# A seven-product down projection: two sets of slots, weight parts parked in device memory, activations split per pair of k

## The chip, the cores and the metric

The kernel runs on one core of a Trainium2 chip, in one launch. The metric is the device time of that launch in microseconds; three runs of the kernel before are known. The core's engines are named as in the profile: PE (TensorE, with PEld for its weight loads), DVE (VectorE), ACT (ScalarE), POOL (GpSimd) and SP (SyncE), which here only issues DMAs.

## The reference

Two post-norm layers on a sequence of 256 positions with 2048 features, all in float32. Layer 0 mixes tokens with a gated spatial unit (gMLP), layer 1 with latent attention (MLA); a gated FFN with a causal convolution follows each.

```python
for i in range(DEPTH):                         # DEPTH = 2
    m = gmlp_mixer(x, ...) if i % 2 == 0 else mla_mixer(x, ...)
    x = layer_norm(ALPHA * x + m, ln_mix_g[i], ln_mix_b[i])
    f = conv_ffn(x, ffn_w_up[i], ffn_conv_w[i], ffn_conv_b[i], ffn_w_down[i])
    x = layer_norm(ALPHA * x + f, ln_ffn_g[i], ln_ffn_b[i])

def conv_ffn(x, w_up, conv_w, conv_b, w_down):  # w_up 2048 x 11008, w_down 5504 x 2048
    h = causal_depthwise_conv3(x @ w_up, conv_w) + conv_b
    a, g = jnp.split(h, 2, axis=-1)
    return (jax.nn.silu(g) * a) @ w_down
```

The gMLP's input projection is 2048 x 12288 (half of it u, half v), its output projection 6144 x 2048.

## The kernel before

**Products.** PE multiplies numbers of the type float32r. To keep float32's accuracy, every operand x is split into hi = x rounded to float32r (a copy on ACT) and lo = x - hi (a subtraction on DVE), and a product is three matmuls: hi by hi, lo by hi, hi by lo (prod_b, L284).

**Eight or seven products.** In the projections v, wo (the gMLP's output) and dn (an FFN's down projection), the weights come in chunks of one pair of k (two blocks of 128 rows) by 1024 columns, 1 MB. Both blocks of 128 positions use them, so a pair is a product of 2 x 2 blocks of activations by 2 x 2 blocks of weights (128 x 512). A "wide" pair does it in eight products (Banks.eight, L341), 24 matmuls. A "seven" pair does it in seven (Banks.seven, L348), 21 matmuls, with sums of weight blocks (ts, made on DVE at L122) and of activation blocks (combine, L209). Four banks (OWN) collect results that Banks.rest (L358) adds up after the last such pair of a half or group; the four others (DIRECT) take the rest.

**Order.** Feed (L69) owns the weights: a list of chunks in order of use. next() (L142) returns the split parts of one chunk, and before that issues loads up to four chunks ahead and splits up to two ahead. Loads go through SP's queue in that order. A wide chunk takes three slots (raw, wh, wl), a seven six (raw, ts, wh, wl, th, tl).

**Slots.** One set of 22 slots of 128 x 2048 words, "big", holds nearly everything: weights, the activations between the stages (pT and act, 8 k to a slot), their split parts, the split layer input (xhl, four slots), the residual (res, two slots), g and b of the norms. A slot is given back after its last use; who wants one waits. Smaller buffers are "t1" (8 of them) and "t2" (6).

**Stages.** v (6 groups of 8 chunks), u (12 groups of 4) with the gate, wo (2 halves of 24 pairs); a boundary: norm, transposes and the first group of the next product, while the last three or four chunks of the old one are still multiplied (boundary, L471); up (86 chunks in 22 groups), dn (2 halves of 22 units, the last of which is a single k), a boundary, MLA, a boundary, and up and dn of layer 1. BACK (L56) lists which pairs of wo and dn are sevens (7 and 6 a half) and the order of the second half. Sums (L370) makes the split activations, four k at a time (quad), and for a seven its four combinations (make), which serve both halves.

Of the kernel before, what the change touches and what calls it, by code (L numbers as in the profile page):

```python
# [8 lines left out]
F32 = mybir.dt.float32  # L9
# [6 lines left out]
P = 128  # L16
S = 256
# [42 lines left out]
def halves(n_k):  # L60

    one = [tuple(range(k, min(k + 2, n_k))) for k in range(0, n_k, 2)]
    two = []
    for q in BACK[n_k][1]:
        two += one[2 * q : 2 * q + 2][:: -1 if q in BACK[n_k][2] else 1]
    return [one, two]


class Feed:  # L69
# [3 lines left out]
    def __init__(self, nc, pool, chunks):  # L73
        self.nc, self.pool, self.chunks = nc, pool, chunks
# [19 lines left out]
    def _split(self):  # L94
        i = self.split
        cols, kind = self.chunks[i][1:]
# [5 lines left out]
        hi = self.pool.tile([P, 2048], F32R, tag="big", name=f"wh{i}")  # L102
        lo = self.pool.tile([P, 2048], F32R, tag="big", name=f"wl{i}")
# [14 lines left out]
    def _seven(self, i, raw):  # L118
# [4 lines left out]
        tile = lambda name, dt: self.pool.tile([P, 2048], dt, tag="big", name=f"{name}{i}")  # L123
# [8 lines left out]
        return wh, wl, th, tl  # L132

# [16 lines left out]
def trunk(ctx: ExitStack, tc: tile.TileContext, x, xT, gm_in, gm_wout, ffn_up, ffn_dn,  # L150
# [4 lines left out]
    big = ctx.enter_context(tc.tile_pool(name="big", bufs=22))  # L155
# [4 lines left out]
    def slot(shape, name, dt=F32):  # L160
        return big.tile(shape, dt, tag="big", name=name)
# [8 lines left out]
    chunks = []  # L170
# [6 lines left out]
    def back(w, n_k):  # L177

        for hf, units in enumerate(halves(n_k)):
            c = slice(hf * 1024, (hf + 1) * 1024)  # L180
            for u in units:
                if len(u) == 1:
                    chunks.append((w[u[0], :, c], 1024, "wide"))
                else:
                    chunks.append((w[u[0] : u[0] + 2, :, c].rearrange("k p c -> p k c"), 2048,
                                   "seven" if u[0] in BACK[n_k][0] else "wide"))

# [972 lines left out]
```

## Time and profile before

| | |
|---|---|
| median of 3 runs | 2493.01 us (2491.49 to 2493.38) |
| profiled execution | 2493.04 us, its span 2491.3 us |
| PE busy | 2475.7 us, 99% of the span |
| DVE busy | 1908.8 us, 77% |
| ACT busy | 1388.8 us, 56% |
| POOL busy | 2.9 us |
| DMA | 480 MB, 193 GB/s on average |
| granted TensorE clock | 0.999 |

Busy time is a share of the whole span, over stages with different limits; a row of windows gives it for one stage. A row of a group names the code line, the engine, the operation, what it writes from what it reads with the shape, how often it ran, its busy time and the mean of one in ns, and the time that the engine sat idle before it, with what ended that. Matmuls are pipelined, so their means overlap; the time of one is read from a run of them in the chain. A wait names who waited, for whom, and then the microseconds in total, the count and the longest.

### The profile page before, as it was taken

The page shows a single profiled execution, that of the slowest core. Times are in us where ns is not written, and L with a number is a line of the kernel's source. Part 1 is how long each engine was busy: PE and PEld are TensorE (multiplying, and loading weights), DVE is VectorE, ACT ScalarE, POOL GpSimd, SP SyncE. Part 2 cuts the span into 40 slices and gives each one's busy share as a digit, 9 for nine tenths or more (in the row PEclk, how much of TensorE's full clock was granted, in tenths as well). Part 3 has the DMA queues.
Part 4 walks back from the last instruction along what each step waited for, and adds up shares of the span by engine and source line. Part 5 has one row for each costly group of instructions (what it writes and reads, how often), then busy time and mean ns, then how long its engine had stood idle before and what let it go on. Part 6 is the DMA issues. An engine that isn't in the chain of part 4 may idle for free.

```text
span 2491.3 us, 32651 instructions
## 1 busy us (share of the span) xinstructions
PE 2475.7 (99%) x13028; PEld 2128.3 (85%) x13028; DVE 1908.8 (77%) x2553; ACT 1388.8 (56%) x1891; POOL 2.9 (0%) x17
## 2 busy tenths in 40 slices
PE   9999999999999999999999999999999999999998
PEld 7888888888888888888888888988888888888886
DVE  7999866678888777666778997866487676669897
ACT  6566544445565755554655566565565555546553
POOL 0000000000000000000000000000000000000000
PEclk9999999999999999999999999999999999999999
DMA  7555554555566655555546674444465455555554
GB/s 295 198 187 214 196 186 157 181 196 194 186 217 222 223 186 200 188 184 185 187 155 201 219 247 169 168 153 168 156 231 191 169 202 182 180 179 179 209 192 181
DMA packets 86456, 480.27 MB, mean 193 GB/s; under 512 B 7712, under 2 KB 8480, under 8 KB 46752
## 3 DMA queue, kind: packets, MB, share of 16 engines
q1 hardware_dynamic: 86304, 478.19, 54.4%
q8 instruction: 102, 1.67, 0.3%
q14 instruction: 50, 0.41, 0.1%
HBM read 476.07 MB, written 2.10 MB: 192 GB/s over the span
## 4 chain that ended last, share of the span: by engine, by line
PE 96%; DVE 2%; issue 1%; DMA 1%; ACT 0%; SPq 0%; DVEq 0%; ACTq 0%
PE up L167 37%; PE u L167 11%; PE dn_q L167 9%; PE dn_p L167 6%; PE wo_q L167 4%; PE v_q L167 4%; PE mo L167 4%; PE dn_e L167 3%; PE v_p L167 3%; PE wo_p L167 3%; PE upf L167 2%; PE wo_e L167 2%; PE v_e L167 1%; PE mkv L167 1%; PE kn L167 1%; PE mq L167 1%
## 5 line engine op out<-in xcount | busy, mean ns | idle before, releaser
L108 DVE TENSOR_TENSOR wl<-raw,wh 128x1024 fp32r<-128x1024 f32 (+3 forms) x651 | 899.8, 1407 | 158.6 <-ACT wh L107 115.5
L107 ACT CAST wh<-raw 128x1024 fp32r<-128x1024 f32 (+3 forms) x651 | 761.8, 1201 | 284.9 <-DVE wl L108 120.4
L167 PE MATMUL up<-xhl,wh 128*128 128x512 f32 x2624 | 611.0, 390 | 0.0
L167 PEld LDWEIGHTS up<-xhl,wh 128*128 128x128 f32 x2624 | 487.4, 188 | 97.8
L167 PEld LDWEIGHTS up<-xhl,wl 128*128 128x128 f32 x2624 | 325.8, 192 | 6.4
L167 PE MATMUL up<-xhl,wl 128*128 128x256 f32 x2624 | 328.1, 283 | 0.0
L115 ACT CAST th<-ts 128x1536 fp32r<-128x1536 f32 x116 | 121.1, 1051 | 118.6 <-DVE ts L122 103.9
L167 PE MATMUL u<-xhl,wh 128*128 128x512 f32 x768 | 183.8, 393 | 0.3 <-DVE h_u L313 0.2
L167 PEld LDWEIGHTS u<-xhl,wh 128*128 128x128 f32 x768 | 141.3, 188 | 30.8 <-PE s L167 2.1
L116 DVE TENSOR_TENSOR tl<-ts,th 128x1536 fp32r<-128x1536 f32 x116 | 138.6, 1219 | 5.3 <-ACT th L115 4.5
L115 ACT CAST wh<-raw 128x1536 fp32r<-128x1536 f32 x58 | 85.9, 1480 | 43.2 <-DMA raw<-in_ffn_dn_dram 15.2
L116 DVE TENSOR_TENSOR wl<-raw,wh 128x1536 fp32r<-128x1536 f32 x58 | 101.6, 1752 | 5.4 <-ACT wh L115 5.4
L167 PEld LDWEIGHTS u<-xhl,wl 128*128 128x128 f32 x768 | 95.6, 192 | 2.0
L167 PE MATMUL u<-xhl,wl 128*128 128x256 f32 x768 | 96.7, 283 | 0.0
L167 PE MATMUL mo<-wh,oT 128*128 128x512 f32 x256 | 82.9, 404 | 0.0
L122 DVE TENSOR_TENSOR ts<-ts,raw 128x512 f32<-128x512 f32 x116 | 79.8, 688 | 1.8
L167 PE MATMUL wo_q<-wh,woa 128*128 128x512 f32 x256 | 78.8, 389 | 0.0
L122 DVE TENSOR_TENSOR ts<-raw 128x1024 f32<-128x1024 f32 x58 | 70.8, 1220 | 4.6 <-PE u L167 1.6
L313 DVE TENSOR_TENSOR h_0a<-up,lo_0a 128x256 f32<-128x256 f32 x41 | 17.3, 421 | 72.7 <-ACT lo_0a L311 72.7
L313 DVE TENSOR_TENSOR h_1a<-up,lo_1a 128x256 f32<-128x256 f32 x41 | 17.3, 421 | 71.9 <-ACT lo_1a L311 71.9
L167 PE MATMUL dn_q<-wh,dn0a 128*128 128x512 f32 x232 | 71.7, 390 | 0.0
L167 PE MATMUL dn_q<-wh,dn1a 128*128 128x512 f32 x232 | 71.5, 389 | 0.0
(497 smaller groups left out, 3924.6 us busy)
## 6 DMA issues: line engine op xcount, KB each, us to landing
raw<-in_ffn_up_dram SPq DMA_DIRECT2D x172, 1024.0 KB, 4.7
raw<-in_gm_in_dram SPq DMA_DIRECT2D x93, 1024.0 KB, 4.7
raw<-in_ffn_dn_dram SPq DMA_DIRECT2D x84, 1024.0 KB, 5.1
raw<-in_gm_wout_dram SPq DMA_DIRECT2D x48, 1024.0 KB, 5.2
raw<-in_ml_out_dram SPq DMA_DIRECT2D x16, 1024.0 KB, 4.8
raw<-in_ml_b_dram SPq DMA_DIRECT2D x14, 1024.0 KB, 4.8
raw<-in_ml_kv_dram SPq DMA_DIRECT2D x5, 864.0 KB, 4.4
lng<-in_ln_rows_dram SPq DMA_DIRECT2D x4, 1024.0 KB, 5.0
```

The costliest lines, as they stand in the source:

```text
L107: self.nc.scalar.copy(hi[:, c], raw[:, c])
L108: self.nc.vector.tensor_tensor(lo[:, c], raw[:, c], hi[:, c].bitcast(F32), ALU.subtract)
L115: self.nc.scalar.copy(hi, raw)
L116: self.nc.vector.tensor_tensor(lo, raw, hi.bitcast(F32), ALU.subtract)
L122: add = lambda o, a, b: self.nc.vector.tensor_tensor(o, a, b, ALU.add)
L167: nc.tensor.matmul(o, l, r, start=start, stop=stop, skip_group_check=True)
L313: nc.vector.tensor_tensor(h, acc[:, 0:S], lo, ALU.add)
```

## The change

The slots become two sets, 17 "big" and 6 "side". The small set holds the v groups, five of the six pT, the last two act of an FFN, qnT and vv of MLA, and parked weights.

In each FFN down projection, 11 of 22 units of the first half and 9 of the second are now done in seven products. Nine of these 20 are "parked" (p in PLAN): Feed.park makes their sums and splits while the up projection before runs, one step behind each of its chunks from the third group on, and stores the four parts in device memory from POOL's queue. When their turn comes, Feed._load fetches the four parts into the small set, also from POOL's queue, instead of loading and splitting the raw pair. wo keeps seven such pairs a half.

The second half of wo and dn runs through the pairs backwards. Acts replaces Sums: it makes the split activations of one pair at a time, with the sums if the pair is a seven or parked, and keeps them only if they are wanted again within KEEP units. The products within a seven change their order (those on wh and wl come first), as do the pairs in the v groups. The residual no longer stays in SBUF through an FFN: Norm.park stores it while the up projection runs, and Norm.fetch brings back each half eight units before the end of that half. g and b of the inner norms come in quarters into small buffers; t1 has 6 of these, t2 has 5.

```diff
-V_PAIRS = [[0, 1, 2, 3, 4, 5, 6, 7]] + [[2, 0, 3, 1, 4, 5, 6, 7]] * 5
+V_PAIRS = [[0, 1, 2, 3, 4, 5, 6, 7]] + [[0, 2, 1, 3, 5, 4, 6, 7]] * 5
...
-BACK = {NF_GM: ((4, 10, 16, 22, 28, 34, 40), (11, 1, 2, 0, 4, 5, 7, 8, 10, 3, 6, 9), (5, 8)),
-        NF_FF: ((4, 10, 16, 22, 30, 34), (10, 1, 2, 0, 4, 5, 7, 8, 3, 6, 9), ())}
...
+T1, T2 = 6, 5
+SLOTS = {"big": 17, "side": 6}
...
+PLAN = {NF_GM: ("0e 1e 2s 3e 4e 5s 6e 7e 8s 9e 10e 11s 12e 13e 14s 15e 16e 17s 18e 19e 20s 21e 22e 23e",
+                "23e 22e 21s 20e 19e 18s 17e 16e 15s 14e 13s 12e 11e 10s 9e 8e 7s 6e 5s 4e 3e 2e 1e 0e"),
+        NF_FF: ("0e 1e 2s 3e 4p 5s 6e 7p 8s 9e 10p 11s 12e 13e 14s 15p 16e 17s 18e 19p 20e 21e",
+                "21e 20e 19p 18s 17e 16e 15p 14s 13e 12e 11s 10p 9e 8s 7e 6p 5s 4e 3e 2e 1e 0e")}
+KINDS = {"e": "wide", "s": "seven", "p": "parked"}
+KEEP = {"wide": 5, "seven": 24, "parked": 12}
...
-        ap, cols = self.chunks[self.loaded][:2]
-        t = self.pool.tile([P, 2048], F32, tag="big", name=f"raw{self.loaded}")
+        ap, cols, kind = self.chunks[self.loaded][:3]
+        if kind == "parked":
+            self.parts[self.loaded] = self._fetch(self.loaded)
+            self.loaded += 1
+            return
...
+    def park(self, i):
+        name = f"{i}"
+        tile = lambda n, dt: self.pool.tile([P, 2048], dt, tag="side", name=f"{n}{i}", bufs=SLOTS["side"])
+        add = lambda o, a, b: self.nc.vector.tensor_tensor(o, a, b, ALU.add)
+        two = lambda a, o: a[:, o : o + 1024].rearrange("p (n c) -> p n c", n=2)
+        self.kept[i] = kept = {}
+        def store(n, t, cols):
+            d = self.dram.tile([P, cols], F32, tag=f"kept{n}{i}", name=f"kept{n}{i}", bufs=1)
+            self.nc.gpsimd.dma_start(d, t[:, 0:cols].bitcast(F32))
+            kept[n] = d
+        ap = self.chunks[i][0]
+        raw = tile("praw", F32)
+        self.nc.sync.dma_start(raw.rearrange("p (k c) -> p k c", k=ap.shape[1]), ap)
+        yield
+        yield
+        yield
+        t = tile("pts", F32)
+        add(two(t, 0), two(raw, 512), raw[:, None, 0:512].to_broadcast([P, 2, 512]))
+        add(t[:, 1024:1536], t[:, 0:512], raw[:, 1024:1536])
+        add(t[:, 1536:2048], t[:, 1024:1536], raw[:, 1536:2048])
+        yield
+        for n, src, o, cols in (("w", raw, 512, 1536), ("t", t, 0, 2048)):
+            hi, lo = tile(f"p{n}h", F32R), tile(f"p{n}l", F32R)
+            self._cast(hi[:, 0:cols], lo[:, 0:cols], src[:, o : o + cols])
+            store(f"{n}h", hi, cols)
+            store(f"{n}l", lo, cols)
+            if n == "w":
+                del raw, src, hi, lo
+                yield
+    def _fetch(self, i):
+        got = []
+        for n in ("wh", "wl", "th", "tl"):
+            d = self.kept[i].pop(n)
+            t = self.pool.tile([P, 2048], F32R, tag="side", name=f"f{n}{i}", bufs=SLOTS["side"])
+            self.nc.gpsimd.dma_start(t[:, 0 : d.shape[1]], d)
+            got.append(t)
+        return got
...
+                if kind == "parked":
+                    parked.append(len(chunks))
+                chunks.append((w[2 * u : 2 * u + 2, :, c].rearrange("k p c -> p k c"), 2048, kind))
...
+    def turn(t, k1, k2):
+        b0, b1 = slice(0, P), slice(P, S)
+        nc.vector.tensor_tensor(t[:, 0], k1[:, b0], k1[:, b1], ALU.subtract)
+        nc.vector.tensor_tensor(t[:, 1], k1[:, b1], k2[:, b1], ALU.subtract)
+        nc.vector.tensor_tensor(t[:, 2], t[:, 1], k1[:, b0], ALU.subtract)
+        nc.vector.tensor_tensor(t[:, 3], k2[:, b0], t[:, 2], ALU.add)
...
         def seven(self, a, sums, wh, wl, th, tl):
             s1, s2, s3, s4 = sums
+            self.to("q3", s4, wh, wl, 512)
+            self.to("p2", a[0][1], wh, wl, 1024)
             self.to("p1", a[0][0], wh, wl, 0)
+            self.to("q4", a[1][1], th, tl, 1536)
             self.to("q5", s1, th, tl, 0)
             self.to("p7", s3, th, tl, 512)
             self.to("p6", s2, th, tl, 1024)
-            self.to("q3", s4, wh, wl, 512)
-            self.to("p2", a[0][1], wh, wl, 1024)
...
+    class Acts:
+        def __init__(self, src, tag, n_k):
+            self.src, self.tag, self.n_k = src, tag, n_k
+            self.got, self.room = {}, None
+        def make(self, u, kind):
+            if u in self.got and (kind == "wide" or self.got[u][1]):
                 return
+            name, n = f"{self.tag}{u}{kind[0]}", min(2, self.n_k - 2 * u)
+            x = self.src[u // 4][:, 2 * u % 8 : 2 * u % 8 + n, :]
+            if kind == "wide":
+                if self.room is None:
+                    self.room = slot([P, 4, 512], f"{name}x", F32R)
+                    t = self.room[:, 0:n]
+                else:
+                    t, self.room = self.room[:, 2 : 2 + n], None
+                hi, lo = t[:, :, 0:S], t[:, :, S : 2 * S]
+                sums = None
+            else:
+                r = slot([P, 2, 8 * P], f"{name}x", F32R)
+                flat = [r[:, h].rearrange("p (s c) -> p s c", s=8) for h in range(2)]
+                hi, lo = [r[:, h, 0 : 4 * P].rearrange("p (k c) -> p k c", k=2) for h in range(2)]
+                t = tp.tile([P, 4, P], F32, tag="t2", name=f"{name}t", bufs=T2)
+                turn(t, x[:, 0], x[:, 1])
+                nc.scalar.copy(flat[0][:, 4:8], t)
+                nc.vector.tensor_tensor(flat[1][:, 4:8], t, flat[0][:, 4:8].bitcast(F32), ALU.subtract)
+                sums = [(flat[0][:, 4 + i], flat[1][:, 4 + i]) for i in (1, 2, 0, 3)]
+            nc.scalar.copy(hi, x)
+            nc.vector.tensor_tensor(lo, x, hi.bitcast(F32), ALU.subtract)
+            parts = [[(hi[:, j, b * P : (b + 1) * P], lo[:, j, b * P : (b + 1) * P]) for j in range(n)]
+                     for b in range(2)]
+            self.got[u] = (parts, sums)
...
+        seq = plan(n_k)
+        line = seq[0] + seq[1]
+        late, at = [], 0
+        for hf, units in enumerate(seq):
...
+                for v2 in line[at : at + 3]:
+                    acts.make(*v2)
+                if i == n - 8:
+                    ln.fetch(hf)
...
+                elif kind == "wide":
+                    acc.eight(a, *got)
+                else:
+                    acc.seven(a, sums, *got)
...
+                at += 1
+                for v2 in [v2 for v2 in acts.got if not any(v2 == w2 and n2 < KEEP[kind2]
+                                                            for n2, (w2, kind2) in enumerate(line[at:]))]:
+                    acts.got.pop(v2)
...
+        def fetch(self, h):
+            if h in self.res:
+                return
+            t = slot([P, 2, 1024], f"res{self.idx}_{h}")
+            for b in range(2):
+                src = x[b * P : (b + 1) * P, h * 1024 : (h + 1) * 1024] if self.away is None else self.away[h][:, b, :]
+                nc.sync.dma_start(t[:, b, :], src)
+            self.res[h] = t
...
+        def park(self, h):
+            d = dram.tile([P, 2, 1024], F32, tag=f"res{self.idx}_{h}", name=f"resd{self.idx}_{h}", bufs=1)
+            nc.gpsimd.dma_start(d, self.res.pop(h))
+            self.put_away[h] = d
...
+        def restore(self, f):
+            row = []
+            for j in range(2):
+                t = tp.tile([P, 512], F32, tag="t2", name=f"lnp{self.idx}_{f}{j}", bufs=T2)
+                src = ln_rows[2 * self.idx + j : 2 * self.idx + j + 1, f * 512 : (f + 1) * 512]
+                nc.sync.dma_start(t, src.to_broadcast([P, 512]))
+                row.append(t)
+            for b in range(2):
+                nc.vector.tensor_tensor(self.r(b, f), self.r(b, f), row[0], ALU.mult)
+                nc.vector.tensor_tensor(self.r(b, f), self.r(b, f), row[1], ALU.add)
...
-        vt = slot([P, 2, 1024], f"v{gi}")
+        vt = slot([P, 2, 1024], f"v{gi}", tag="side")
...
-            pT[sl] = slot([P, 8, S], f"pT{sl}")
+            pT[sl] = slot([P, 8, S], f"pT{sl}", tag="side" if sl else "big")
...
+    def park_all(until):
+        for i in [i for i in parked if feed.used < i < until]:
+            yield from feed.park(i)
+            yield
...
-                act[a // 8] = slot([P, 8, S], f"act{layer}_{a // 8}")
+                act[a // 8] = slot([P, 8, S], f"act{layer}_{a // 8}", tag="side" if a // 8 > 3 else "big")
...
+        xhl, old = ln.new, ln
+        jobs = park_all(feed.used + 2 * n_up)
...
+                if gi > 1:
+                    next(jobs, None)
...
-            if gi == 21:
-                sums.first()
...
-            if gi == 1:
-                ln.rows()
-            if 3 <= gi < 11:
-                ln.restore((gi - 3) // 4, (gi - 3) % 4)
+            if 1 < gi < 6:
+                old.restore(gi - 2)
+            if gi in (4, 6):
+                old.park(gi // 2 - 2)
+            if gi == 19:
+                for t in plan(NF_FF)[0][:2]:
+                    acts.make(*t)
             if gi == 20:
-                for k in BACK[NF_FF][0][:2]:
-                    sums.make(k)
-        ln = Norm(2 * layer + 1, res, last)
-        return (ln, *down(NF_FF, act, f"dn{layer}", ln, sums, 4 if last else SKEW))
+                acts.make(*plan(NF_FF)[0][2])
+        ln = Norm(2 * layer + 1, {}, old.put_away, last)
+        return (ln, *down(NF_FF, act, f"dn{layer}", ln, acts, 4 if last else SKEW))
...
+    vv = [slot([P, D], f"vv{b}", tag="side") for b in range(2)]
```

More of the change, by code (lines that the diff above doesn't have):

```diff
@@ L177, in back @@
     def back(w, n_k):
-        for hf, units in enumerate(halves(n_k)):
+        for hf, units in enumerate(plan(n_k)):
             c = slice(hf * 1024, (hf + 1) * 1024)
[L181 to L186, printed above, removed]
+            for u, kind in units:
+                if 2 * u + 1 == n_k:
+                    chunks.append((w[2 * u, :, c], 1024, kind))
+                    continue
+                if kind == "parked":
+                    parked.append(len(chunks))
+                chunks.append((w[2 * u : 2 * u + 2, :, c].rearrange("k p c -> p k c"), 2048, kind))
     back(gm_wout, NF_GM)
@@ L714, in trunk @@
         if gi == 10:
-            for k in BACK[NF_GM][0][:2]:
-                sums.make(k)
-    ln = Norm(0, None)
-    acc, end = down(NF_GM, pT, "wo", ln, sums)
+            acts.make(*plan(NF_GM)[0][2])
+    ln = Norm(0, {})
+    acc, end = down(NF_GM, pT, "wo", ln, acts)
     def conv(layer, F, acc, name):
@@ L859, in trunk @@
         if 1 <= c < 5:
[L860 to L861 removed]
+            ln.restore(c - 1)
     kr2 = []
```

192 lines of the change are left out of this document (66 added, 126 removed).

## The prediction

> **What bounds the kernel now.** I read the page first, then the busy time by stage, the chain in order of time, and the groups by shape.
>
> ```profile
> span 2491.3 us, 32651 instructions
> PE 2475.7 (99%) x13028; PEld 2128.3 (85%) x13028; DVE 1908.8 (77%) x2553; ACT 1388.8 (56%) x1891; POOL 2.9 (0%) x17
> PE 96%; DVE 2%; issue 1%; DMA 1%; ACT 0%; SPq 0%; DVEq 0%; ACTq 0%
> ```
>
> ```profile
> core 0: us, PE busy (x) PEld busy (x) DVE busy (x) ACT busy (x) POOL busy (x), PEclk, DMA share, GB/s
> 549.00:805.00 256.00, 254.82 (x1127) 210.34 (x1126) 223.01 (x215) 144.18 (x126) 0.00 (x0) 1.00 0.60 204
> 805.00:836.00 31.00, 31.00 (x164) 25.82 (x163) 19.00 (x24) 24.07 (x46) 0.00 (x0) 1.00 0.57 197
> 836.00:1287.00 451.00, 451.00 (x2594) 399.18 (x2593) 316.17 (x483) 246.57 (x371) 0.00 (x0) 1.00 0.53 189
> 1287.00:1508.00 221.00, 221.00 (x979) 182.89 (x978) 197.09 (x186) 126.19 (x105) 0.32 (x2) 1.00 0.61 205
> ```
>
> The windows are the output projection of the gMLP ("wo"), the boundary behind it, and the up and down projections of FFN 0. TensorE is busy in all of each window but wo's (1.2 us idle), and the chain that ended last is 96% TensorE. So the end moves by what the matmuls take, as long as the other engines and DMA keep ahead of them. Two covers are thin already: VectorE is busy 89% of the down projection, 87% of wo.
>
> ```profile
> 1289.14 2.72 PE dn_q L167 x12
> 1300.02 2.04 PE dn_q L167 x9
> 1493.18 5.44 PE dn_q L167 x24
> ```
>
> These pieces of the chain give the price of one 512-wide product step: 12 matmuls in 2.72 us, 0.2267 us each. A pair of k done in eight products is 24 matmuls, 5.44 us; one done in seven is 21, 4.76 us.
>
> **The change, part by part.** *Fewer matmuls.* Each FFN down projection did 6 pairs per half in seven products, 24 over two halves and two layers. The new plan has 6+5 of 22 units in the first half ("s" and "p") and 5+4 in the second, 40 over both layers. So 16 x 3 x 0.2267 = **-10.9 us**, all on TensorE. wo (7 and 7) and the v groups (4 of 8) keep their numbers.
>
> *Order of the v groups.* A group now begins with a pair in eight products, on banks that the group before gave up with its last "seven", not on those that its last sum reads.
>
> ```profile
> L167 PE MATMUL v_q<-wh,xc 128*128 128x512 f32 x40 | 12.6, 395 | 0.8 <-DVE v L637 0.8
> ```
>
> That wait, 0.8 us in all, should go: **-0.8** (bounds -0.8 and 0; late next would be VectorE, which has the two sevens 4 and 6 in a row).
>
> *VectorE and ScalarE.* The prices:
>
> ```profile
> L108 DVE TENSOR_TENSOR wl<-raw,wh 128x2048 fp32r<-128x2048 f32 x119 | 271.4, 2288 | 33.5 <-ACT wh L107 31.1 <-PE dn_q L167 1.0 <-ACT th L115 0.8
> L107 ACT CAST wh<-raw 128x2048 fp32r<-128x2048 f32 x119 | 226.8, 1912 | 62.8 <-DVE wl L108 12.3 <-PE wo_q L167 10.6 <-PE dn_q L167 10.6
> L116 DVE TENSOR_TENSOR tl<-ts,th 128x1536 fp32r<-128x1536 f32 x58 | 101.7, 1753 | 5.3 <-ACT th L115 4.5
> L116 DVE TENSOR_TENSOR wl<-raw,wh 128x1536 fp32r<-128x1536 f32 x58 | 101.6, 1752 | 5.4 <-ACT wh L115 5.4
> L115 ACT CAST wh<-raw 128x1536 fp32r<-128x1536 f32 x58 | 85.9, 1480 | 43.2 <-DMA raw<-in_ffn_dn_dram 15.2 <-PE dn_p L167 11.0 <-DVE wl L108 5.5
> L122 DVE TENSOR_TENSOR ts<-ts,raw 128x512 f32<-128x512 f32 x116 | 79.8, 688 | 1.8
> L122 DVE TENSOR_TENSOR ts<-raw 128x1024 f32<-128x1024 f32 x58 | 70.8, 1220 | 4.6 <-PE u L167 1.6 <-DMA raw<-in_gm_wout_dram 1.1 <-DMA raw<-in_ffn_dn_dram 1.0
> L116 DVE TENSOR_TENSOR tl<-ts,th 128x512 fp32r<-128x512 f32 x58 | 39.7, 685 | 0.0
> L395 DVE TENSOR_TENSOR dn0a<-act,dn0a 128x1024 fp32r<-128x1024 f32 x19 | 23.2, 1219 | 3.5 <-ACT dn0a L394 3.4
> L220 DVE TENSOR_TENSOR dn0xc<-xsdn,dn0xc x6: 681/686/693, 1278.6 to 1362.6; 128x512 fp32r<-128x512 f32 x6
> L217 DVE TENSOR_TENSOR xsdn<-act,xsdn x12: 281/284/294, 903.9 to 2289.3; 128x128 f32<-128x128 f32 x12
> ```
>
> Splitting a "wide" pair costs VectorE 2.29 us, a "seven" 1.22 + 2 x 0.69 + 1.75 + 1.75 + 0.69 = 6.79. In a down projection, wide pairs go from 30 to 22 and sevens split there from 12 to 11: -25.1 us. The parts of the activations were 19 fours of k at 1.22, four single k at 0.69 and 6 combinations at 4 x 0.28 + 0.69 = 1.82, together 36.9. By the new KEEP rule I count 22 wide makes at 0.69 and 17 with sums at 4 x 0.28 + 2 x 0.69 = 2.51, together 57.8: +20.9. Net -4 of 197 in a stage 5 us shorter: still 89%. In wo nothing is parked and the same count gives 32 wide and 14 with sums, 57.1 for 42.3: 238 of 255 us, 93%.
>
> ```profile
> 138.00:179.00 41.00, 40.61 (x179) 33.28 (x179) 38.84 (x37) 26.13 (x33) 0.00 (x0) 1.00 0.54 204
> ```
>
> A v group runs at 95% VectorE with 0.39 us of TensorE idle, so 93% is taken at **0** (bounds 0 and the added 15 us).
>
> ```profile
> 834.95 450.10 PE up L167 x2592
> ```
>
> The parking lies beside the up projection (81 chunks of 32 matmuls in 450.10 us, 5.56 each): nine pairs at 2.60 (sums) + 1.75 + 2.29 = 6.64 us of VectorE, 59.7, so 376 of 451 us (83%); ScalarE gets 9 x (1.48 + 1.91) = 31, so 277 (61%). TensorE has two chunks in hand there; if that cover went, a chunk would wait for at most one such cast, 2.3 us. The parked pair's raw load goes through SP, ahead of the raw loads of the next chunks; if it had to wait for a slot of the small set they would wait too. At most five of six are in use then (raw is given back before the next pair's is asked for), and the ninth pair is through (54 chunks of 78) before the activations take two. Cost **0**.
>
> *DMA.*
>
> ```profile
> 30.00:38.00 8.00, 8.00 (x37) 6.64 (x36) 8.00 (x9) 7.18 (x7) 0.00 (x0) 1.00 1.01 425
> L83 SPq DMA_DIRECT2D raw<-in_ffn_dn_dram x84: 367/368/422, 1257.3 to 2448.0; - x84
> DMA to landing us min/median/max: 4.9/5.1/9.4
> SPq L83 <- PE dn_q L167: 212.3, 40, 10.9
> ```
>
> The first row is the rate that the queues hold when full, 425 GB/s (1.05 MB in 2.5 us); the others are the issue and landing of a raw load of 1.05 MB in the down stage, and SP waiting for a slot. A parked pair's four parts (128 rows of 1536, 1536, 2048 and 2048 words) are 3.67 MB, stored and fetched. In the up stage the load and store of nine add 42.5 MB in 451 us: 189 to 283 GB/s, hidden. A down projection goes from 45 MB to 45 - 9.4 + 33.0 + 2.1 (residual) = 71 MB in 216 us, 329 GB/s, 77% of 425.
>
> The fetches are issued on POOL's queue, where nothing else is queued in that stage, so a wait there blocks no raw load on SP. But the small set has 6 slots, and until the third unit of the second half the last activations hold two. So parts of pair 7 can only start when pair 4's are used up: wh and wl after 9 matmuls (2.04 us), th and tl after 21 (4.76 us). With p, s, e between the starts, 4.76 + 4.76 + 5.44 = 14.96 us, th and tl have 14.96 - 4.76 + 2.04 = 12.2 us to land. Two alone need 5.1 + 2.5 = 7.6 us; with both raw loads of that period (2 x 2.5 us) in between, 12.6. Places this tight are 4 to 7, 7 to 10 and 15 to 19 in the first half, six in two layers; in the second half freed slots give a lead. The trace has no DMA from POOL and none into a float32r tile. Bounds: nothing late, or each of the two landing after the slowest 9.4 us, one behind the other, 6.6 late x 6 = 40. I take 0.5 each, **+3.0**, near the median landing.
>
> The Trainium skill ("DMA: Bandwidth & Descriptors", Specifications) gives a core about 358 GB/s from HBM; by that the period's 5.77 MB would take 16.1 us and each tight fetch would come 1.2 us late, an estimate of +7 us in all. The trace disagrees for loads, at 425 GB/s.
>
> *Slots.* 17 for 22 in the big set. In the first down half, four hold activations, 3 to 6 their parts, one the residual: 6 to 10 are left for weights, and parked pairs take none.
>
> ```profile
> 549.00:676.00 127.00, 127.00 (x562) 105.16 (x561) 111.89 (x116) 72.40 (x63) 0.00 (x0) 1.00 0.61 202
> ```
>
> wo's first half had 22 less 6 (pT), 2 (res), 3 (activations' parts) and 4 (combinations), 7 left at its fullest, and lost nothing. At a boundary six hold the late weights, two parts, two the residual: 7 left, of which the new xhl needs 4. Bounds: 0, or at three boundaries a load that starts only when a slot frees, 5.1 + 1.91 + 2.29 - 5.44 = 3.9 us late each, 11.6. I take **+1.0**, near the boundary row (31.00 of 31.00).
>
> *The rest*: the residual stored beside each up stage and fetched eight units before the end of each half (2.1 MB each way, in the figures above but for the store), rows of g and b in quarters, fewer small buffers (8 to 6, 6 to 5): 0, under the same slack of VectorE and DMA; if a small buffer is missing, one 0.7 us operation.
>
> **Sum.** -10.9 - 0.8 + 3.0 + 1.0 = -7.7. The profiled execution took 2493.04 us (span 2491.3 and 1.7 around it); the median of the runs is 2493.01, so both give **2485.3 us**. Without any stall it is 2481.3; 2488 with 6.7 us of stalls. That is this case's own range.
>
> **Rivals.** *1, the fetches eat the gain.* If a tight period's whole 5.77 MB passes after the slot frees, it takes 13.6 + 2.6 (the part of a landing that is not transfer) = 16.2 us of 14.96: 1.3 late x 6 = 7.8. -11.7 + 7.8 + 1.0 gives **2490.1**. For it: 91% of the measured rate is wanted there. Against it: the average is 77%.
> *2, slower: POOL's fetches are slow.* They go into float32r from float32, a conversion that no DMA of before does. At half rate, 3.67 MB takes 17.4 us and the period 22.4: +7.4 at the six tight places; the looser gaps (16.3 to 25.2 us) lose 2 to 9 each, about 88 in all: **2570**. It decides from about 310 GB/s downwards, where six periods of 11.8 + 5.0 us lose 11. For it: nothing in the trace shows the rate; against: the bytes are plain rows of 6 and 8 KB.
> *3, slower: the big set is too small where stages meet.* Seven places (three boundaries, two starts of a down projection, two turns of its halves) at 3.9 us: 27, **2511**. From three places on, the gain is gone. For it: SP waits 212 us for dn_q's slots already; against: the row of 549 to 676.
>
> **Chances.** Forecast 0.56, rival 1 0.20, rival 2 0.10, rival 3 0.12, others 0.02. A measurement tells about 0.2%, 5.0 us. Faster 0.57, same 0.20, slower 0.23. The range leaves out rival 2 and the worse half of rival 3: 2480.5 to 2505.
>
> **What the profile would show.** Right: dn matmuls fewer by 48; down stages 5 us shorter each with TensorE full; a POOL queue of some 130 MB beside q1; up stages at 450 us with VectorE near 376; no wait of a v matmul on DVE. Wrong: TensorE idle on DMA into the fetched parts at pairs 7, 10, 19 (rival 1), at every parked pair and over 12 us a landing (rival 2), or on wh or wl behind SP's slot waits at boundaries (rival 3).

## The result, and the profile after

The changed kernel takes 2577.6 us (median, 2576.76 to 2579.69) beside 2492.9 us of the kernel before on the same chip: ratio 1.0342, 95% interval 1.0324 to 1.0360. It is 84.7 us slower, where 7.7 us faster was forecast.

The profiled execution after, from the page (busy time; DMA queues with packets, MB and share of the engines' time):

```profile
span 2574.8 us, 33461 instructions
PE 2492.3 (97%) x12980; PEld 2133.2 (83%) x12980; DVE 2006.6 (78%) x2810; ACT 1433.2 (56%) x1984; POOL 82.3 (3%) x165
q1 hardware_dynamic: 90336, 482.39, 52.6%
q0 software_dynamic: 21312, 136.32, 13.3%
```

13028 - 12980 = 48 matmuls have gone, as forecast. Yet PE is busy 16.6 us longer than before (2492.3 to 2475.7), and idle for 82.5 us of the span, before 15.6. So two things went wrong: PE waits, and its matmuls are slower. The rows of one tile tell where. Each gives the shortest, median and longest duration in ns and the first and last start. First the kernel before, then the changed one:

```profile
L167 PE MATMUL up<-xhl,wh x1312: 387/389/402, 826.3 to 1284.7; 128*128 128x512 f32 x188
L167 PE MATMUL dn_q<-wl,dn0a x116: 387/389/396, 1301.0 to 1511.0; 128*128 128x512 f32 x116
L167 PE MATMUL up<-xhl,wh x1312: 389/389/398, 1793.4 to 2254.6; 128*128 128x512 f32 x188
L167 PE MATMUL dn_q<-wl,dn1a x116: 388/389/389, 2270.9 to 2480.4; 128*128 128x512 f32 x116
```

```profile
L222 PE MATMUL up<-xhl,wh x1312: 387/389/796, 835.0 to 1313.8; 128*128 128x512 f32 x188
L222 PE MATMUL dn_q<-wh,dn01wx x16: 388/389/393, 1531.2 to 1546.4; 128*128 128x512 f32 x16
L222 PE MATMUL up<-xhl,wh x1312: 388/389/792, 1843.4 to 2329.6; 128*128 128x512 f32 x188
L222 PE MATMUL dn_q<-wh,dn11wx x16: 389/389/450, 2547.1 to 2563.3; 128*128 128x512 f32 x16
```

From last start to last start: up to the end of up in layer 0, 1284.7 before and 1313.8 after; down 226.3 and 232.6; to the end of up in layer 1, 743.6 and 783.2; down 225.8 and 233.7. I call the first and third stretches together the front: 2028.3 before, 2097.0 after, **68.7 us lost**. The two down projections went from 452.1 to 466.3; with 10.9 us of matmuls less they should have come to 441.2, so **25.1 us are lost there**. 68.7 + 25.1 - 10.9 = 82.9 of the 83.5 us by which the span is longer.

Where in the front? The windows of the changed kernel, columns as in the prediction (busy time of each engine, the clock, DMA share, GB/s), and then one of the kernel before:

```profile
549.00:805.00 256.00, 252.98 (x1114) 208.17 (x1112) 237.67 (x266) 152.69 (x146) 4.93 (x9) 1.00 0.71 249
805.00:841.00 36.00, 30.84 (x136) 24.85 (x136) 30.76 (x38) 28.71 (x52) 4.69 (x9) 0.86 0.76 275
841.00:960.00 119.00, 106.47 (x589) 93.51 (x588) 96.75 (x137) 67.60 (x90) 8.70 (x17) 0.95 0.91 348
960.00:1314.00 354.00, 354.00 (x2040) 313.62 (x2039) 252.59 (x379) 196.87 (x293) 4.29 (x8) 1.00 0.60 220
```

```profile
830.00:950.00 120.00, 120.00 (x698) 106.50 (x697) 95.80 (x144) 71.70 (x104) 0.00 (x0) 1.00 0.59 210
```

In the output projection PE is idle for 3.0 us (1.2 before). At the boundary and in the first 119 us of up it has long gaps and a lower clock. For the other 354 us of up it is full, and there DMA is busy 60%, for 53% over the whole of up before. 8.70 us of POOL's 12.99 in up fall into the first 119 us: the parking isn't spread over the stage. (Layer 1 has the larger part of the loss, 39.6 of the 68.7 us.)

Its loads show the same. The row of the parked pairs' raw loads, for the time up to 835.0, when up's first wide product starts:

```profile
L160 SPq DMA_DIRECT2D praw<-in_ffn_dn_dram x5: 367/379/410, 549.4 to 828.1; - x5
```

Five of nine were issued before up began, the first some 300 us before up's third group; in layer 1 six of nine were. The program asks one by one, from up's third group on. But the order within each engine's queue is made by a planner. As I read it, it lets an instruction go first when the one ahead of it has no slot: with one set of slots a parked pair would have stood in line; with a set of its own it finds a slot free while the weights' loads wait for the big set, and passes them (parking with one set of slots wasn't tried).

What that does, at one of the long gaps: SP's queue, ScalarE and PE in order of time, with the wait of SP at the parked load's slot (in brackets: idle time before, and what ended it; a row of several issues holds the time between them).

```profile
920.27 0.33 SPq L96 DMA_DIRECT2D raw<-in_ffn_up_dram  x1
920.77 0.38 SPq L160 DMA_DIRECT2D praw<-in_ffn_dn_dram  x1
924.11 0.33 SPq L96 DMA_DIRECT2D raw<-in_ffn_up_dram  x1
936.52 15.62 SPq L160 DMA_DIRECT2D praw<-in_ffn_dn_dram  x2
952.24 3.67 SPq L96 DMA_DIRECT2D raw<-in_ffn_up_dram  x3
```

```profile
947.01 1.49 ACT L126 CAST pwh<-praw 128x1536 fp32r<-128x1536 f32 x1 [8.44 <-DMA praw<-in_ffn_dn_dram]
952.43 1.90 ACT L126 CAST pth<-pts 128x2048 fp32r<-128x2048 f32 x1 [0.39 <-DVE pts L149]
954.81 1.04 ACT L118 CAST wh<-raw 128x1024 fp32r<-128x1024 f32 x1
```

```profile
946.14 3.81 PE L222 MATMUL up<-xhl,wh 128*128 128x512 f32 x16
955.90 6.32 PE L222 MATMUL up<-xhl,wh 128*128 128x512 f32 x16 [5.95 <-ACT wh L118]
```

```profile
954.00:961.00 7.00, 5.09 (x12) 3.98 (x13) 6.64 (x10) 5.49 (x10) 1.06 (x2) 0.52 0.97 300
```

```profile
SPq L160 <- DMA kepttl<-ptl: 14.7, 1, 14.7
```

A parked load leaves at 936.52 and lands 10.4 us later, on DMA engines that are 95% busy. ScalarE stands idle for 8.44 us of that with the load's cast at the head of its queue. The wh that PE needs is behind it (its raw load left at 924.11 or before, and that one took 10.7 us to land; the next left at 952.24, too late for a cast at 954.81), so PE gets it at 955.90, 5.95 us late. Then the clock is at half: the same 16 matmuls take 6.32 us for 3.81. Meanwhile SP waits 14.7 us for a slot of the small set, which a store holds until it has landed, and from 924.11 to 952.24 no load of up's weights is issued.

The Trainium skill ("TensorE: Matmul & The Clock Gate", Architectural detail) says that ScalarE and VectorE run their queues in strict order. These rows agree: a cast whose load had landed waited behind one whose load had not.

There are longer gaps, and they show that this is not the only way. First the longest of layer 0, with the window in front of it, then the longest of all, in layer 1:

```profile
861.90 1.99 ACT L118 CAST wh<-raw 128x1024 fp32r<-128x1024 f32 x2 [5.17 <-DMA raw<-in_ffn_up_dram]
864.25 3.78 PE L222 MATMUL up<-xhl,wl 128*128 128x256 f32 x16 [6.58 <-DVE wl L119]
858.00:864.00 6.00, 0.00 (x0) 0.00 (x0) 1.35 (x2) 2.10 (x3) 0.00 (x0) 0.84 1.00 416
```

```profile
1964.56 1.90 ACT L126 CAST pth<-pts 128x2048 fp32r<-128x2048 f32 x1 [6.23 <-DMA keptth<-pth]
1968.03 3.66 PE L222 MATMUL up<-xhl,wh 128*128 128x512 f32 x8 [11.64 <-ACT wh L118]
```

At 864 no parked cast is in the way: a weight load, issued at 847.0 behind five row loads, took 14.9 us to land on full DMA engines. At 1968 ScalarE stood 6.23 us at a parked cast, not for its load but for a small slot that a store still held. At the boundaries, where PE waits for the norm (3.56 and 1.60 us in layer 0, 6.96 and 1.61 in layer 1), VectorE has parked sums and differences between the norm's steps.

### The profile page after: what moved, and what is told of

It is laid out like the page before. It is cut to its first block, busy times and chain, and to the rows that moved or that the text cites. A ratio compares the mean times of both kernels' runs of the same rounds, so it can differ in the third digit from the quotient of the medians.

```text
span 2574.8 us, 33461 instructions
## 1 busy us (share of the span) xinstructions
PE 2492.3 (97%) x12980; PEld 2133.2 (83%) x12980; DVE 2006.6 (78%) x2810; ACT 1433.2 (56%) x1984; POOL 82.3 (3%) x165
## 3 DMA queue, kind: packets, MB, share of 16 engines
q1 hardware_dynamic: 90336, 482.39, 52.6%
q0 software_dynamic: 21312, 136.32, 13.3%
## 4 chain that ended last, share of the span: by engine, by line
PE 47%; issue 37%; DMA 9%; DVE 5%; ACT 1%; POOL 1%; SPq 0%; DVEq 0%; POOLq 0%; ACTq 0%
PE u L222 10%; PE v_q L222 4%; PE wo_q L222 4%; PE dn_q L222 3%; DMA raw<-in_ffn_dn_dram 3%; PE v_p L222 3%; PE wo_p L222 3%; PE dn_p L222 3%; PE mo L222 2%; PE up L222 2%; PE wo_e L222 2%; PE v_e L222 1%; DVE wl L119 1%; DMA raw<-in_ffn_up_dram 1%; DMA fwh<-keptwh 1%
## 5 line engine op out<-in xcount | busy, mean ns | idle before, releaser
L119 DVE TENSOR_TENSOR wl<-raw,wh 128x1024 fp32r<-128x1024 f32 (+3 forms) x635 | 867.2, 1384 | 266.0 <-ACT wh L118 207.1
L118 ACT CAST wh<-raw 128x1024 fp32r<-128x1024 f32 (+3 forms) x635 | 734.0, 1182 | 439.7 <-DVE wl L119 137.3
L222 PE MATMUL up<-xhl,wh 128*128 128x512 f32 x2624 | 619.0, 393 | 20.3 <-ACT wh L118 20.3
L127 DVE TENSOR_TENSOR tl<-ts,th 128x1536 fp32r<-128x1536 f32 x112 | 133.2, 1216 | 2.0 <-ACT th L126 1.7
L126 ACT CAST wh<-raw 128x1536 fp32r<-128x1536 f32 x56 | 82.9, 1481 | 60.1 <-DMA raw<-in_ffn_dn_dram 25.6
L222 PE MATMUL mo<-wh,oT 128*128 128x512 f32 x256 | 82.9, 404 | 3.7 <-DVE oT L1081 3.7
L222 PE MATMUL v_q<-wh,xhl 128*128 128x512 f32 x224 | 69.9, 392 | 2.4 <-ACT wh L118 2.4
L222 PE MATMUL v_p<-wh,xhl 128*128 128x512 f32 x192 | 59.8, 389 | 0.0
L222 PEld LDWEIGHTS mo<-wh,oT 128*128 128x128 f32 x256 | 45.5, 189 | 11.3 <-DVE oT L1081 4.1
L222 PEld LDWEIGHTS v_q<-wh,xhl 128*128 128x128 f32 x224 | 42.1, 189 | 12.0 <-ACT wh L118 3.5
L127 DVE TENSOR_TENSOR ptl<-pts,pth 128x2048 fp32r<-128x2048 f32 x18 | 41.1, 2284 | 13.5 <-DMA kepttl<-ptl 9.3
## 6 DMA issues: line engine op xcount, KB each, us to landing
keptth<-pth POOLq DMA_DIRECT2D x18, 1024.0 KB, 10.4
```

Of the source, the lines that this page charges most:

```text
L118: self.nc.scalar.copy(hi[:, c], raw[:, c])
L119: self.nc.vector.tensor_tensor(lo[:, c], raw[:, c], hi[:, c].bitcast(F32), ALU.subtract)
L126: self.nc.scalar.copy(hi, raw)
L127: self.nc.vector.tensor_tensor(lo, raw, hi.bitcast(F32), ALU.subtract)
L222: nc.tensor.matmul(o, l, r, start=start, stop=stop, skip_group_check=True)
```

## The experiments

Three theories at first. *Order*: the planner puts parked loads ahead of weights, and PE starves. *Traffic*: the parking's bytes cost wherever they lie. *Slots*: 17 big slots, the stored residual or the rows of g and b cost by themselves.

All runs together, each beside the kernel before on the same chip (2492.9 to 2493.5 us). "Front" and "down" are worked out from last starts as above, against the kernel before; "down" is cleared of the matmuls saved or added (0.2267 us each), so that it is stalls alone.

| run | matmuls | median us | ratio to before (95%) | front lost | down lost |
|---|---|---|---|---|---|
| changed kernel | 12980 | 2577.6 | 1.0342 (1.0324 to 1.0360) | 68.7 | 25.1 |
| e1 no parking | 13034 | 2493.9 | 1.0005 (0.9995 to 1.0014) | -1.3 | 0.3 |
| e2 parked loads held in place | 12980 | 2508.6 | 1.0064 (1.0049 to 1.0079) | 0.6 | 25.4 |
| e3 rows of g and b held too | 12980 | 2518.6 | 1.0102 (1.0086 to 1.0119) | 8.4 | 26.6 |
| e4 parked loads on POOL's queue | 12980 | 2573.5 | 1.0328 (1.0313 to 1.0343) | 67.5 | 29.1 |
| e7 no stores | 12980 | 2545.6 | 1.0203 (1.0187 to 1.0220) | 22.6 | 39.0 |
| e8 traffic without splits | 12980 | 2532.5 | 1.0161 (1.0148 to 1.0175) | 22.5 | 26.9 |
| e6 as e2, 16 big slots | 12980 | 2532.1 | 1.0152 (1.0137 to 1.0168) | 19.4 | 32.7 |
| e12 as e2, one fetch a stage | 12980 | 2481.6 | 0.9955 (0.9938 to 0.9971) | -0.7 | -0.6 |
| e5 as e2, no parking at the turn | 13004 | 2495.5 | 1.0010 (1.0001 to 1.0019) | -0.6 | 6.8 |
| e9 as e2, four parked a layer | 13010 | 2489.6 | 0.9983 (0.9974 to 0.9992) | -0.2 | 0.6 |
| e10 as e2, six parked a layer | 12998 | 2502.7 | 1.0041 (1.0028 to 1.0053) | -0.7 | 14.9 |
| e11 as e9, loads left to the planner | 13010 | 2517.1 | 1.0100 (1.0084 to 1.0115) | 27.6 | -0.4 |

### e1: no parking

```diff
-... 3e 4p 5s 6e 7p 8s 9e 10p 11s 12e 13e 14s 15p 16e 17s 18e 19p 20e 21e"
+... 3e 4e 5s 6e 7e 8s 9e 10e 11s 12e 13e 14s 15e 16e 17s 18e 19e 20e 21e"
```

(and the second half in the same way)

> The nine parked pairs of each layer are done as wide pairs (eight products), everything else stays: 17 and 6 slots, the residual stored and fetched, g and b in quarters, the second half backwards. 22 sevens for the 24 of the kernel before are 6 matmuls more, +1.4 us. If the parking (its loads, stores, splits and fetches) makes the loss: 2490 to 2505 us. If 17 slots, the stored residual or the rows of g and b make it: 2530 us or more, with TensorE idle at the same boundaries.

Measured: 2493.9 us, 1.0 above the kernel before, with 6 matmuls (1.4 us) more. The theory of slots falls: 17 slots, the residual stored and fetched, the rows in quarters, the activations pair by pair and the second half backwards cost nothing that can be measured, as long as nothing is parked.

### e2: parked loads held in their place in SP's queue

```diff
-        self.nc.sync.dma_start(raw.rearrange("p (k c) -> p k c", k=ap.shape[1]), ap)
+        with self.tc.issue_after(self.last.ins):       # last: the raw load issued before
+            self.nc.sync.dma_start(raw.rearrange("p (k c) -> p k c", k=ap.shape[1]), ap)
```

> Each parked pair's raw load is held in SP's queue behind the raw load that stands before it in the program (an edge of order, no wait), so that the nine come evenly over the up stage's first 54 chunks and none in the output projection or at the boundary. Same bytes, same instructions. If the order of SP's queue (parks bunched ahead of weights where few weights are in hand) makes the loss: most of the 85 us come back, 2485 to 2515 us. If the parking's traffic as such makes it: 2550 us or more. If slots or the rows of g and b make it: 2530 us or more.

Measured: 2508.6 us. The front is whole again (0.6 us), with the same bytes and matmuls. The row of the loads, and the windows of up:

```profile
L162 SPq DMA_DIRECT2D praw<-in_ffn_dn_dram x18: 378/382/1157, 851.8 to 2097.0; - x18
```

```profile
831.00:951.00 120.00, 120.00 (x698) 106.48 (x697) 108.37 (x155) 76.92 (x104) 7.57 (x14) 1.00 0.92 338
951.00:1286.00 335.00, 335.00 (x1929) 296.61 (x1928) 264.92 (x382) 199.37 (x285) 14.90 (x28) 1.00 0.78 286
```

The first 120 us move 338 GB/s with the DMA engines 92% busy, nearly what they do in the changed kernel (348, 91%), and PE loses nothing. So the order decides, and DMA engines 92% busy don't by themselves. Spread out, the parked work also waits less: for their loads ScalarE waited 5.7 us and VectorE 6.9 over the whole run, 32.1 and 25.0 in the changed kernel. What is left, 15.7 us over the kernel before, is nearly all in the down projections.

### e3: the rows of g and b held too

```diff
-                nc.sync.dma_start(t, src.to_broadcast([P, 512]))
+                with tc.issue_after(feed.last.ins):
+                    nc.sync.dma_start(t, src.to_broadcast([P, 512]))
```

> As the run before, and the loads of the rows of g and b are held behind the weight loads in the same way. If these rows, issued five in one go at the boundary in front of two weight loads, cost by themselves: 5 to 20 us below the run with only the parked loads held. If they only share in a jam that the parks make: within 3 us of it.

Measured: 2518.6 us, 10 us above e2 where the same or less was expected. The row of VectorE before the longest gap:

```profile
925.06 1.29 DVE L622 TENSOR_TENSOR res<-res,lnp 128x512 f32<-128x512 f32 x2 [7.39 <-DMA lnp<-in_ln_rows_dram]
932.82 3.92 PE L224 MATMUL up<-xhl,wh 128*128 128x512 f32 x16 [2.86 <-ACT wh L119]
```

Held back, the rows come in the middle of the parked pairs' traffic, and a 256 KB row arrives after VectorE has reached the work on it. VectorE waits 7.39 us, all its later work with it, and PE 2.86. It is the same mechanism with another load: what counts is how long before its reader a load is issued. These rows are better early.

### e4: the parked loads on POOL's queue

```diff
-        self.nc.sync.dma_start(raw.rearrange("p (k c) -> p k c", k=ap.shape[1]), ap)
+        self.nc.gpsimd.dma_start(raw.rearrange("p (k c) -> p k c", k=ap.shape[1]), ap)
```

> The parked pairs' raw loads are issued from POOL's queue instead of SP's; their place in time is left to the planner, as in the changed kernel. If the loss is SP's queue standing still while a parked load waits for a slot of the small set (104 us of such waits): 2500 to 2535 us. If it is the bunched traffic on the DMA engines: 2560 to 2580 us.

Measured: 2573.5 us, the front as bad as before (67.5). That SP's queue stands behind the parked loads doesn't explain the loss: without it the front loses as much. The parking is still bunched (the first load now at 550.3), and its loads take longer to land (14.7 us for 8.7, medians).

### e7: no stores, and e8: the traffic without the splits

e7, on the changed kernel's order; the fetches read the same bytes from the input:

```diff
-            store(f"{n}h", hi, cols)
-            store(f"{n}l", lo, cols)
...
-            d = self.kept[i].pop(n)
+            d = self.chunks[i][0][:, :, 0 : 768 if n[0] == "w" else 1024]
...
```

> The changed kernel without the 72 stores of parked parts: the splits are made and dropped, and the down projection fetches the same number of bytes from the input weights instead, so its numbers are wrong. SP's queue keeps the changed kernel's order (parked loads at the same 18 places, give or take two). If the bunched loss is the DMA engines being full (stores are 3.67 of the 4.7 MB that a parked pair moves there, and hold the small slots until they land): 2510 to 2535 us. If it is VectorE's and ScalarE's queues standing behind a parked pair's load, or SP's: 2560 to 2580 us.

e8; each parked load is held behind the weight load that it followed in the changed kernel (that edge isn't in the cut):

```diff
-        t = tile("pts", F32)
-        add(two(t, 0), ...)     # the sums, and below the four casts and differences
...
-            store(f"{n}h", hi, cols)
-            store(f"{n}l", lo, cols)
+            store(f"{n}h", src, cols)     # src: the loaded pair itself
+            store(f"{n}l", src, cols)
```

> The changed kernel without the sums and splits of the parked pairs (9 x 6.6 us of VectorE and 9 x 3.4 us of ScalarE per layer gone): each parked pair is loaded behind the same weight load as in the changed kernel, and stored four times straight from the loaded pair, the same bytes; its numbers are wrong. If full DMA engines at the boundary and in the first 120 us of up make the bunched loss of 69 us: 2550 to 2575 us. If it takes VectorE's and ScalarE's queues, held up by a parked pair that has not landed, to turn late bytes into idle TensorE: 2510 to 2535 us.

Measured: 2545.6 and 2532.5 us, the one between the two expectations, the other where the queues were blamed. In the front, where each leaves out one part of the parking, both lose the same: 22.6 and 22.5 of 68.7. The windows of 841 to 960, e7 first:

```profile
841.00:960.00 119.00, 116.21 (x677) 102.62 (x676) 110.64 (x155) 77.81 (x106) 1.23 (x2) 1.00 0.71 265
```

```profile
841.00:960.00 119.00, 118.74 (x685) 105.00 (x684) 87.17 (x135) 63.98 (x93) 10.57 (x20) 1.00 0.87 353
```

With all the parking's work, and without the three quarters of its bytes that are stores (265 GB/s), PE loses 2.8 us there; with all the bytes (353 GB/s) and none of the work, 0.3. In the changed kernel it loses 12.5 idle, and more through its clock. Neither explains the 68.7 us alone: take either away and 46 of them go. So most of the loss takes both, the bytes and the parked work on VectorE and ScalarE; the rows of 955.90 show how, late bytes and work that waits for them ahead of the weights' splits. What remains lies mostly at the boundaries (PE's waits for the norm: 3.56, 1.99 and 4.71 us in e7, 3.03, 2.15 and 4.75 in e8). The two runs don't part everything: a small slot held by a store, as at 1968, goes in both, since e7 has no stores and e8 takes one slot a pair where the changed kernel takes up to five. How much that makes of the 46 us stays open. (In e7's down projections the fetch reads shorter rows and lands later, ftl after 14.3 us for 10.4, so that column isn't used.)

### e12 and e6: what the down projections lose

e12, on e2: one fetch in each down projection.

```diff
+        self.fetched = getattr(self, "fetched", -1) + 1
+        if self.fetched % 9:
+            got = self.held            # given up after the ninth
+            return got
-        got = []
+        got = self.held = []
```

> As the run with the parked loads held in place, but in each down projection only the parts of the first parked pair are fetched; the eight others use them again, so the numbers are wrong. All nine are still loaded, split and stored in the up stage; matmuls, plan and the 17 and 6 slots stay. 8 x 3.67 MB fewer cross the DMA engines in each down projection. If the fetches' bytes make the 25 us that the two down projections lose: 2481 to 2487 us. If the 17 slots, the activations' parts or the order backwards make them: 2500 to 2510 us.

Measured: 2481.6 us. Nothing is lost any more, and the down projections come to 220.6 and 220.0 us, for 220.9 and 220.4 by the matmuls. The page and the rows:

```profile
PE 2464.2 (99%) x12980; PEld 2119.1 (85%) x12980; DVE 2006.2 (81%) x2810; ACT 1432.5 (58%) x1984; POOL 47.7 (2%) x101
```

```profile
L230 PE MATMUL up<-xhl,wh x1312: 388/389/402, 826.0 to 1284.4; 128*128 128x512 f32 x188
L230 PE MATMUL dn_q<-wh,dn01wx x16: 389/389/397, 1490.0 to 1505.0; 128*128 128x512 f32 x16
```

With the same 12980 matmuls the changed kernel's PE was busy 2492.3 us: 28.1 us of its loss are slower matmuls, and 67.0 us are idle time (82.5 less the 15.5 that e12 has, in a span of 2479.7).

In e2, with all nine fetched, the turn between the halves looks like this, and the raw loads' landing in that down projection (e2 first, then e12):

```profile
1390.00:1430.00 40.00, 35.11 (x146) 27.64 (x145) 31.21 (x54) 14.02 (x13) 3.53 (x7) 0.96 0.97 370
```

```profile
DMA to landing us min/median/max: 4.8/8.5/14.1
```

```profile
DMA to landing us min/median/max: 4.7/6.4/8.6
```

DMA is 97% busy, and a raw load takes up to 14.1 us for 8.6. Ten fetches are issued in the 31 us from 1387.5 to 1418.2. The wide pairs 21 and 16 behind the turn are split late; PE waits for the splits there, not for fetched parts. (e12 takes away the bytes of eight fetches and their waits for slots at once, and doesn't part the two.)

e6, on e2:

```diff
-SLOTS = {"big": 17, "side": 6}
+SLOTS = {"big": 16, "side": 6}
```

> As the run with the parked loads held in place, with 16 big slots for 17. If what is left of the loss there (27 us over the forecast) comes from raw loads that wait for a slot: 10 us or more on top, 2519 to 2540 us. If it comes from full DMA engines alone: 2507 to 2513 us.

Measured: 2532.1 us, 23.5 above e2; in the profiled executions 26.2, of which 7.3 in the down projections and 18.8 in the front. So beside the parking the big set can't be smaller: with 17 the front of e2 loses nothing and e12 nothing anywhere, with 16 the front loses in both layers (16 without parking wasn't tried). In the down projections, as I read it, slots and bytes act together (a late load keeps its slot, and the next load waits for one), but with 17 it is the fetches that start it: e12 has the same slots.

### e5, e9, e10, e11: fewer parked pairs

All with e2's edge, but for e11. e5: pairs 15 and 19 wide in both halves. e9: parked are 4 and 10 in the first half, 15 and 10 in the second. e10: 16 and 6 as well.

> As the run with the parked loads held in place, and pairs 15 and 19, the two on both sides of the turn between the halves, are wide in both halves: 10 parked pairs left of 18, 24 matmuls more (8 x 3 x 0.2267 = +5.4 us). If the stalls at the turn (wl of pairs 21 and 16, wh of 16, in both layers some 7 us with the halved clock behind them) come from the fetches' bytes and slots: 2508.6 + 5.4 - 14 = 2500 us. If they come from the 17 slots or the turn itself: 2514 us.

Measured: 2495.5 us, 4.5 better than the better of the two numbers: the stalls at the turn have gone, 6.8 us remain, those for ftl of pairs 7 and 10 in the first half among them.

> As the run with the parked loads held in place, with four parked pairs a layer (4 and 10 in the first half, 15 and 10 in the second) and the other five wide: 10 x 3 x 0.2267 = 6.8 us more matmuls than with nine, 5.4 us fewer than with none. If two fetches a half, at least five units apart, find their slots and the DMA engines free: 2493.9 - 5.4 = 2488.5 us, below both kernels. If each parked pair costs what it costs with nine (12.2 + 14.7 us over 18 pairs, 1.5 each): 2493.9 - 5.4 + 12 = 2500 us.

Measured: 2489.6 us, ratio 0.9983 (0.9974 to 0.9992), the fastest full computation here, some 4 us under the kernel before; 18 matmuls fewer are worth 4.1. The page shows PE full:

```profile
PE 2472.0 (99%) x13010; PEld 2124.4 (85%) x13010; DVE 1959.3 (79%) x2730; ACT 1414.8 (57%) x1966; POOL 39.3 (2%) x85
```

> As the run with four parked pairs a layer, with six (4, 10 and 16 in the first half, 15, 10 and 6 in the second): 12 fewer matmuls, -2.7 us. If the fetches, at least four units apart, still come in time: 2489.5 - 2.7 = 2486.8 us. If the third fetch of a half brings stalls back: 2492 to 2500 us.

Measured: 2502.7 us, 13 above e9 with 12 matmuls less. One more fetch next to the turn, pair 16, brings the stalls back, at wh and wl of pair 19 in both layers. I take it that what counts is less the number of parked pairs (e5 has ten over both layers and loses 6.8, e10 twelve and 14.9) than how many fetches and raw loads want to pass in the same 30 us. The runs change number and place together, so that is argued, not shown.

> As the run with four parked pairs a layer, but their loads are left to the planner, which puts them at the first four of the changed kernel's places, in the output projection and at the boundary. If the place alone costs, in proportion to the pairs: 4/9 of 69 us, about 31, 2520 us. If it takes the jam of all nine: 2490 to 2500 us.

e11 is e9 without the edge: 2517.1 us, 27.5 above e9, all of it in the front. Place alone costs with four pairs a layer too, about in proportion to nine.

## Why the prediction was wrong

**Fewer matmuls, -10.9: right.** e12 against the kernel before: PE busy 11.5 us less, down projections 11.5 us shorter.

**v groups, -0.8; the rest, 0: right within what e1 can tell** (2493.9, where +1.4 - 0.8 gives 2493.5). No v matmul waits for DVE's v any more in the changed kernel.

**VectorE and ScalarE in up: right in size.** Forecast 376 us of VectorE in up; e2's two windows have 108.37 + 264.92 = 373.3, at no cost to PE. In wo 238 us were forecast; e1 and e2, in which nothing else lies there, have 229 us in the same window and lose nothing.

**The parking at 0: this is the step that failed, by 68.7 us.** "The parking lies beside the up projection" and "hidden" at 283 GB/s are true of e2, where the loads are held there (338 and 286 GB/s in its two windows), and not of the changed kernel. I took the place of each step from the program's text. The code hands the order to a planner, and nothing holds these loads in line; one edge of order brings the front from 68.7 us lost to 0.6. That an average is met says nothing when the work is bunched: 348 GB/s in 119 us, 220 in the other 354.

Two smaller parts of this step were wrong too. "At most five of six are in use then" left out that a slot is held until its store has landed (median us in the last column of the changed kernel's page):

```profile
keptth<-pth POOLq DMA_DIRECT2D x18, 1024.0 KB, 10.4
```

SP did wait there, 14.7 us at the longest, and ScalarE 6.23 at the longest gap. And "a chunk would wait for at most one such cast, 2.3 us" priced the cast as work; as a wait it cost 8.44 us of ScalarE and 5.95 of PE, and then the clock.

**DMA, +3.0: too small, 25 us.** The ceiling of 40 had been worked out; I took a value near the lower end, by the median landing. For the waits that it named the term was about right: PE's gaps for ftl at the tight places 7 and 10 are 0.47, 1.17 and 2.48 us, 4.1 in all. What the sum had no term for is larger. Raw loads made late by the fetches had wide pairs split late (PE waits 10.9 us for splits in the changed kernel's down projections), and PE is busy 10.8 us longer there than in e12, its matmuls slower behind the gaps. "In the second half freed slots give a lead" looked at the small set only: the lead lets ten fetches into 31 us at the turn.

**Slots, +1.0: about right at 17** (e1 and e12 show none), with nothing to spare (e6).

**The rivals.** Rival 1 names the fetches that the down projections suffer from, at a third of the loss (its "1.3 late" is 1.2 by its own terms, 7.4 us in all). Rival 2's 2570 us is near the result by accident: nothing runs at half rate. On the page POOL's queue, half stores and half fetches, took 13.3% of the engines' time for 136.32 MB (0.098% a MB), SP's 52.6% for 482.39 MB (0.109%). Rival 3's place, the boundaries, was right in part and its cause wrong: e2 has the same slots and no loss there. The case that came, the parking's own order, was not among them.

## What to carry to other kernels

Where a planner makes the order, look for what keeps a new load in its place: with a set of slots of its own it need not wait where the others wait. Before a step is costed at nothing beside a long stage, ask which edge holds it there, and give it one; then keep its load well ahead of its reader, since a reader that waits stops everything behind it on its engine. Bytes that fit on average need a look at the fullest 30 us.

## What was not expected of the hardware

Short gaps cost twice. Of the 95.1 us that the changed kernel lies above e12, 28.1 are longer PE busy time, at a granted clock of 0.986 over the run for 0.999: behind some gaps the clock stands near half (0.52 in the window of 954 to 961). A gap of 2.61 us did it in e3, while one of 2.94 us in e2 did not (each row is followed by the windows behind its gap; the clock is third from the end):

```profile
2327.42 0.78 PE L224 MATMUL dn_q<-ftl,dn110px 128*128 128x512 f32 x1 [2.61 <-DMA ftl<-kepttl]
2327.00:2331.00 4.00, 3.58 (x9) 2.86 (x10) 0.87 (x2) 1.90 (x1) 0.00 (x0) 0.57 1.07 422
```

```profile
2319.39 0.50 PE L224 MATMUL dn_q<-ftl,dn110px 128*128 128x512 f32 x1 [2.94 <-DMA ftl<-kepttl]
2319.00:2324.00 5.00, 4.61 (x20) 3.85 (x21) 3.20 (x4) 2.12 (x2) 1.07 (x2) 1.00 1.10 413
2324.00:2329.00 5.00, 5.00 (x23) 4.14 (x23) 4.98 (x7) 3.81 (x4) 0.00 (x0) 1.00 1.02 388
```

The Trainium skill ("TensorE: Matmul & The Clock Gate", What's actually happening) tells of a free-running window of about 3.4 us, with half the clock after at least one idle window. That the longer gap went free and the shorter didn't fits a window that doesn't start with the gap; that a gap shorter than the window suffices does not fit an idle window in the strict sense, and there the measurement holds.

Loads and fetches together passed at 413 to 422 GB/s in the windows with the gaps, little less than the 425 of loads alone before.
